# A layer norm in two operations of VectorE, in place of three on ScalarE, GpSimd and VectorE

## The chip, the cores and the metric

The kernel runs on one core of a Trainium2 chip. The time is that of one execution on the device, in microseconds (us); for a kernel on one core it is that core's time. TensorE multiplies matrices into PSUM; VectorE (DVE in the profile), ScalarE (ACT) and GpSimd (POOL) work on tiles in SBUF; SyncE (SP) issues nearly all DMA transfers here. Every engine takes its instructions strictly in the order in which the program lists them: an instruction that waits holds up all that stand behind it on its engine, and that holds for SP's transfers too.

## The reference, cut to what matters

Two groups of tokens ("p", 1024 rows, and "s", 512 rows, each of 1024 channels) go through two layers. A layer is a mixer (attention with a gate), an output projection, and a layer norm over the residual sum:

```python
def _layernorm(h, g, b):
    mu = jnp.mean(h, axis=-1, keepdims=True)
    var = jnp.mean(jnp.square(h - mu), axis=-1, keepdims=True)
    return (h - mu) * lax.rsqrt(var + LN_EPS) * g + b

for l in range(DEPTH):                      # DEPTH = 2
    ...
    u = x * (1 + scale) + shift             # per channel
    y = mixer_a(u, ...) if l == 0 else mixer_b(u, ...)      # ends in (att * silu(z)) @ w_out
    x = _layernorm(DEEPNORM_ALPHA * x + gate * y, ln_g[l], ln_b[l])
```

All is float32. Only the last line's norm is touched by the change.

## The kernel before, in words

The program runs its stages one after the other: layer 0's attention of "s" and of "p", layer 0's output projection of both (`out_layer(0, ...)`, 1805 to 1990 us of the profile), layer 1's attention of both, and layer 1's output projection (`out_layer(1, ...)`, 2560 us to the end). TensorE works through a list of *groups*, each of 24 matmuls into one of two PSUM buffers (`pj`, two buffers: group n + 2 can't start before group n has been taken out of its buffer). Float32 precision comes from splitting each operand into a rounded part and a rest, `hi` and `lo`, hence three matmuls per 128 channels.

In an output projection the rows are cut in 12 *blocks* of 128 rows: block 0 to 3 are "s", 4 to 11 are "p". A block has two groups, c = 0 and c = 1, for the two halves of the 1024 output channels (the first two blocks run crosswise: 0, 1, 0, 1). What belongs to a block:

- `load` (L1033): a DMA of 512 KB, the block's gated attention output, from the scratch tensor `g_s` or `g_p`;
- `split` (L1046, L1047): ScalarE makes `hi`, then VectorE `lo`; TensorE needs both for the block's groups;
- `load_x` (L1037): a DMA of 512 KB, the residual input `x`;
- the *evacuation* of each group by VectorE: y = a * gate (L1070, reads PSUM and so frees it), x = ALPHA x + y (L1071), statistics (L1072);
- the layer norm of the whole block, once both halves are there: `stat` (L1078 to L1086: VectorE joins the statistics to mean and variance `mv`; four tiny operations of GpSimd make rstd in `mv[:, 1:2]` and -mean x rstd in `nm`), `norm` (L1090, ScalarE: x rstd + nm), `scale` (L1094: x g) and `shift` (L1098: x + b). Of even blocks GpSimd does `scale` and VectorE `shift`, of odd ones the other way round;
- the store of the block (L1100), on SP's queue, to the scratch `x_s`, `x_p` after layer 0 (`x_in[r, 1]`) and to the outputs after layer 1. The store waits for `shift`.

The order on every engine is set by *slots*. TensorE's list has six slots per group: one after each four matmuls, and one after the evacuation is listed. `after(n, f)` lists f's work n slots later; `spread(tasks, n)` lists one task of a list per slot. Before a block's first group, `ahead_of(j)` (L1131) sets off, for block j: x of block j + 1 two slots later, the split of block j + 1 five slots later, and the load of block j + 2 eight slots later. After its second group, `then(j)` (L1147) sets off the list of `finish` (L1105), in which `None` is an empty slot; block 0's list has extra empty slots, since the rows g and b of the norm (`ROW`) are loaded in the second step.

In layer 0 block 3's list goes on with the input of layer 1 for "s": `u_make` (L271) transposes all four "s" blocks on TensorE (L275), 128 channels at a time, then ScalarE (L278, L267) and GpSimd (L269) scale and split them. These transposes stand among the matmuls of the groups and need the finished norm of block 3.

Into the first blocks of each output projection falls the end of the last head pair of "p": a small load of factors `f_p` (L767), products with them (L774 on VectorE and L773 on GpSimd in layer 0, L776 in layer 1), L781, L782, the last part of block 4's split (L1053, L1054) and the store L788 of `g_p`, which the loads of blocks 5 to 11 wait for.

The last block of layer 1 has a list of its own, `finish_last` (L1113), in two halves of 512 channels, all on ScalarE and VectorE.

Of the kernel before, what the change touches and what calls it, by code (L numbers as in the profile page):

```python
# [10 lines left out]
F32 = mybir.dt.float32  # L11
F32R = mybir.dt.float32r
AF = mybir.ActivationFunctionType
ALU = mybir.AluOpType

D = 1024
# [59 lines left out]
def trunk(ctx: ExitStack, tc: tile.TileContext, x_p, x_s, c_p, c_s, w_mod, b_mod, ln_g, ln_b,  # L76
          w_in_a, w_out_a, w_in_b, w_out_b, sink_b, pat_d, id_d, y_p, y_s):
    nc = tc.nc
    PSUM = bass.MemoryType.PSUM
    const = ctx.enter_context(tc.tile_pool(name="const", bufs=1))  # L80
    wk = ctx.enter_context(tc.tile_pool(name="wk", bufs=2))
# [44 lines left out]
    def after(n, f):  # L126
        delayed.append((now[0] + n, f))
# [11 lines left out]
    def spread(tasks, slots):  # L139

        q = Queue(tasks, slots)
        queues.append(q)
        return q
# [94 lines left out]
    def u_alloc(r, l, h=None):  # L238

        if h is None:  # L240
            for part in range(2):
                for k in range(NK):
                    U[r, l, part, k] = slabs.get(F32R)
        else:
            for k in range(NK):
                U[r, l, h, k] = slabs.get(F32R, (128, 2, 512))
# [24 lines left out]
    def u_make(r, l, h, k, xs, b0=0):  # L271
        n = len(xs)
        t = ps_t.tile([128, 4, 128], F32, tag="t", name="t")
        for b in range(n):
            nc.tensor.transpose(t[:, b, :], xs[b][:, k * 128:(k + 1) * 128], ident)  # L275
        s = wk.tile([128, 512], F32, tag="stg", name="ustg")[:, :128 * n]
        m = modT[l][:, REQ[r], :]
        nc.scalar.activation(s, t[:, :n].rearrange("p b t -> p (b t)"), AF.Identity,  # L278
                             bias=m[:, k:k + 1], scale=m[:, 8 + k:9 + k])
        u_split(r, l, k, s, 512 * h + 128 * b0, 128 * n)  # L280
# [18 lines left out]
    def chunk(srcs, groups, pre=None, post=None, deep=0, keep=None, how="pool"):  # L299


        plan.append((range(len(loads), len(loads) + len(srcs)), groups, pre, post, deep, keep))
        loads.extend((src, how) for src in srcs)
# [710 lines left out]
    ROW = {}  # L1014

    def load_row(name, ap):
        ROW[name] = slabs.get()
        nc.sync.dma_start(ROW[name], ap.partition_broadcast(128))

    def free_rows(*names):  # L1020
        slabs.put(*(ROW.pop(n) for n in names))

    class Block:
# [54 lines left out]
        def stat(self):  # L1078
            P = nc.gpsimd
            self.mv = mv = wk.tile([128, 2], F32, tag="mv", name="mv", bufs=4)  # L1080
            self.nm = nm = wk.tile([128, 1], F32, tag="nmr", name="nmr", bufs=4)
            nc.vector.bn_aggr(mv, self.s6)
            P.tensor_scalar(nm, mv[:, 0:1], -1.0, 1.0, ALU.mult, ALU.mult)
            P.tensor_scalar(mv[:, 1:2], mv[:, 1:2], EPS, None, ALU.add)
            P.tensor_tensor(mv[:, 1:2], mv[:, 1:2], mhalf, ALU.pow)
            P.tensor_tensor(nm, nm, mv[:, 1:2], ALU.mult)  # L1086

        def norm(self, cs=slice(0, D)):
            x = self.x[:, cs]
            nc.scalar.activation(x, x, AF.Identity, bias=self.nm, scale=self.mv[:, 1:2])  # L1090

        def scale(self, engine, cs=slice(0, D)):
            x = self.x[:, cs]
            engine.tensor_tensor(x, x, ROW["g"][:, cs], ALU.mult)  # L1094

        def shift(self, engine, cs=slice(0, D)):
            x = self.x[:, cs]
            engine.tensor_tensor(x, x, ROW["b"][:, cs], ALU.add)  # L1098
            out = y_out[self.r] if self.l else x_in[self.r, 1]
            nc.sync.dma_start(out[self.t, cs], x)  # L1100

# [2 lines left out]

        def finish(self):  # L1105

            V, P = nc.vector, nc.gpsimd
            e = (V, P) if self.b % 2 else (P, V)
            keep = (self.r, self.l) == ("s", 0)
            return [self.stat, None, None, None, self.norm, None, lambda: self.scale(e[0]), None, None,  # L1110
                    lambda: self.shift(e[1])] + ([] if keep else [self.free])

        def finish_last(self):  # L1113
            V, P = nc.vector, nc.gpsimd
            self.stat()
            parts = [slice(0, 512), slice(512, 1024)]
            for cs in parts:
                self.norm(cs)
            for cs in parts:
                self.scale(V, cs)  # L1120
                self.shift(V, cs)
            self.free()

    def out_layer(l, first, p0):

        w = (w_out_a if l == 0 else w_out_b)[0]
        W = []
        blocks = first + [Block("s", l, b) for b in (2, 3)] + [p0] + [Block("p", l, b) for b in range(1, 8)]
        n = len(blocks)

        def ahead_of(j):  # L1131

            def f():
                if j + 1 < n:
                    after(2, blocks[j + 1].load_x)
                    after(5, (lambda: p0.split(NP - 1)) if blocks[j + 1] is p0 else blocks[j + 1].split)
                if j + 2 < n:
                    k = blocks[j + 2]
                    if k is p0:
                        after(6, lambda: k.load(0, NP - 1))  # L1140
                        after(9, k.alloc)
                        after(11, lambda: load_row("gatep", gate_d["p", l]))
                    else:
                        after(8, k.load)
            return f

        def then(j):  # L1147
            def f():
                k = blocks[j]
                if l == 1 and j == n - 1:  # L1150
                    k.finish_last()
                    return
                t = k.finish()
                if j == n - 1:
                    t.append(lambda: free_rows("g", "b", "gatep"))
                if l == 0 and j == 3:
                    t += [None, lambda: u_alloc("s", 1, 0)]
                    t += [lambda c=c: u_make("s", 1, 0, c, [b.x for b in blocks[:4]]) for c in range(NK)]
                    t.append(lambda: [b.free() for b in blocks[:4]])
                t = [None] * (8 if j == 0 else 1) + t  # L1160
                spread(t, len(t))
                if j == 3:
                    free_rows("gates")
            return f

        def tiles(c):
            return [[(0, 512, w[256 * i:256 * i + 256, 512 * c:512 * c + 512])] for i in range(4)]

        def begin():
            after(1, blocks[1].load_x)  # L1170
            after(8, blocks[2].load)

        def second():
            ahead_of(1)()
            after(11, lambda: load_row("g", ln_g[l]))
            after(11, lambda: load_row("b", ln_b[l]))

        chunk(tiles(0), [blocks[j].group(W, 0, then(j)) for j in range(2)], pre=begin, keep=W, deep=3)
        chunk(tiles(1), [blocks[j].group(W, 1, then(j)) for j in range(2)], pre=second, keep=W, deep=-1)
        for j in range(2, n):  # L1180
            chunk([], [blocks[j].group(W, c, then(j)) for c in range(2)], pre=ahead_of(j), deep=-1,
                  post=(lambda: slabs.put(*(t for p in W for t in p))) if j == n - 1 else None)


    with tc.manual_schedule():
# [133 lines left out]
        for k in range(NK):  # L1319
            t = ps_t.tile([128, 4, 128], F32, tag="t", name="t")  # L1320
# [31 lines left out]
        def shift():  # L1352
            box["m"] = mod_mm(mods[1])

        after(13, shift)
        after(15, lambda: mod_tr(0, 0, box["m"]))
        after(16, whole)
# [35 lines left out]
```

## Time and profile before

| what | value |
|---|---|
| time, median of 3 runs | 2706.53 us (2704.96 to 2712.18) |
| profiled execution, its own time | 2706.52 us |
| span, first to last instruction | 2704.7 us (1.8 us lie around it) |
| mean granted TensorE clock | 0.988 |
| layer norm's full-size operations, ScalarE | L1090: 23 of 128x1024, mean 1244 ns, and 2 of 128x512 |
| on GpSimd | L1094: 12, mean 2451 ns; L1098: 11, mean 2617 ns |
| on VectorE | L1094: 11, mean 1215 ns; L1098: 12, mean 1481 ns; and 2 + 2 of 128x512 |
| GpSimd's tiny ones, 24 each | L1083 696, L1084 300, L1085 630, L1086 328 ns |

How to read it: busy times are per engine and overlap. A row of the timeline gives the start, the duration, the engine, the line of the kernel and what it writes and reads, buffer numbers left out (`s<-s,s` is any slab, `a` a PSUM buffer of a group), `xN` merges N equal instructions that follow each other, and the brackets tell how long the engine was idle before and what ended that. PEclk is the granted share of TensorE's full clock. The windows view gives the busy time of each engine in a stretch, with the number of its instructions.

### The profile page before, as it was taken

Reading aid. Unit: us, or ns where it says so; the run is one execution under the profiler, and the core shown is the slowest. Engines: PE = TensorE matmul, PEld = TensorE weight load, DVE = VectorE, ACT = ScalarE, POOL = GpSimd, SP = SyncE. Lnnn points to the kernel's source line nnn. Section 1 sums busy time; section 2 is a strip of 40 time slices with the busy share of each in tenths; the row PEclk is TensorE's granted clock in tenths of the full one; section 3 lists DMA queues with packets and bytes.
Section 4 is the critical chain, followed back from the end, with each engine's and each line's share of the span. In section 5 each row is a group of like instructions: output and inputs, shape, how many; then the busy total and the mean of one; then the engine's idle time right before and its main releaser. Section 6 shows DMA issues by size and latency. Waiting matters only on the chain.

```text
span 2704.7 us, 39461 instructions
## 1 busy us (share of the span) xinstructions
PE 2610.9 (97%) x15139; PEld 2113.0 (78%) x15139; DVE 1253.9 (46%) x2921; ACT 982.5 (36%) x2359; POOL 945.7 (35%) x662
## 2 busy tenths in 40 slices
PE   7899999999999999999999999999999899999898
PEld 4777778778888887888888888877776678777686
DVE  4533434444243425343433434356645543555666
ACT  3334345543132423233232323242345433444321
POOL 4243334344322323223223231334554531223533
PEclk9899999999999999999999999999999999999999
DMA  8354543333222222122323232335442230211453
GB/s 263 114 147 137 153 98 102 98 98 88 59 56 73 61 56 66 42 66 56 79 56 79 52 75 48 78 118 155 133 135 63 82 91 9 58 47 54 133 170 109
DMA packets 294676, 247.36 MB, mean 91 GB/s; under 512 B 29656, under 2 KB 257880, under 8 KB 294488
## 3 DMA queue, kind: packets, MB, share of 16 engines
q1 hardware_dynamic: 291160, 244.35, 32.2%
q8 instruction: 119, 1.95, 0.3%
q10 hardware_dynamic: 3328, 0.49, 0.1%
q14 instruction: 69, 0.57, 0.1%
HBM read 198.16 MB, written 25.67 MB: 83 GB/s over the span
## 4 chain that ended last, share of the span: by engine, by line
PE 80%; DVE 7%; ACT 4%; issue 3%; POOL 2%; DMA 2%; SPq 0%; ACTq 0%; DVEq 0%; POOLq 0%
PE a L364 62%; PE o L458 6%; PE t L430 5%; PE s L557 2%; PE s L558 2%; DVE nm L416 2%; PE s L562 2%; ACT P L419 1%; DVE P L412 1%; DMA s<-s 1%; POOL s L341 1%; DMA s<-g_s 1%; ACT s L531 1%; DVE s L533 1%; PE t L206 1%
## 5 line engine op out<-in xcount | busy, mean ns | idle before, releaser
L364 PE MATMUL a<-s,s 128*128 128x512 f32 (+1 forms) x9648 | 2128.2, 370 | 23.2 <-POOL s L341 4.7
L364 PEld LDWEIGHTS a<-s,s 128*128 128x128 f32 x9648 | 1615.4, 190 | 317.6 <-issue 29.7
L341 POOL TENSOR_TENSOR s<-s,s 128x1024 fp32r<-128x1024 f32 x211 | 509.7, 2417 | 525.5 <-ACT s L336 258.6
L419 ACT ACTIVATE P<-P,nm 128x256 f32<-128x256 f32 (+2 forms) x576 | 312.3, 543 | 690.4 <-DVE nm L416 677.9
L412 DVE CUSTOM_DVE_ANT_0 P<-s,bias 128x256 f32<-128x256 f32 (+2 forms) x576 | 251.6, 472 | 238.4 <-PE s L558 128.0
L334 POOL TENSOR_SCALAR s<-s 128x1024 fp32r<-128x1024 f32 x139 | 152.5, 1097 | 465.0 <-PE a L364 382.0
L430 PE MATMUL t<-ident,P 128*128 128x128 f32 x1408 | 206.6, 275 | 8.6 <-ACT P L419 3.9
L440 DVE COPY PT<-t 128x256 f32<-128x256 f32 (+3 forms) x320 | 141.7, 447 | 139.8 <-PE t L430 136.9
L533 DVE TENSOR_TENSOR s<-a,s 64x512 fp32r<-64x512 f32 x128 | 109.8, 858 | 203.6 <-ACT s L531 202.5
L430 PEld LDWEIGHTS t<-ident,P 128*128 128x128 f32 x1408 | 166.9, 140 | 44.2 <-ACT P L419 12.2
L458 PE MATMUL o<-PT,s 128*64 128x256 f32 (+1 forms) x1984 | 193.7, 328 | 1.1 <-DVE PT L440 1.1
L458 PEld LDWEIGHTS o<-PT,s 128*64 128x64 f32 x1984 | 118.8, 136 | 87.2 <-issue 49.4
L557 PE MATMUL s<-s,s 128*128 128x256 f32 (+2 forms) x512 | 148.4, 306 | 19.0 <-DVE st L412 18.6
L160 ACT ACTIVATE s<-a 128x128 f32<-128x128 f32 (+2 forms) x147 | 56.0, 407 | 267.1 <-PE a L364 267.0
L558 PE MATMUL s<-s,s 128*128 128x256 f32 (+2 forms) x512 | 144.4, 298 | 3.2 <-DMA s<-s 3.0
L438 ACT ACTIVATE PT<-t 128x256 f32<-128x256 f32 (+3 forms) x320 | 125.9, 398 | 53.1 <-PE t L430 46.9
L542 DVE TENSOR_TENSOR s<-a,s 64x512 fp32r<-64x512 f32 x80 | 77.2, 965 | 132.0 <-ACT s L540 131.0
L557 PEld LDWEIGHTS s<-s,s 128*128 128x128 f32 x512 | 97.7, 191 | 36.7 <-DVE st L412 30.0
L416 DVE TENSOR_SCALAR nm<-st 128x2 f32<-128x2 f32 x288 | 119.0, 413 | 10.0
L162 DVE COPY s<-a 128x128 f32<-128x128 f32 (+2 forms) x105 | 49.4, 491 | 146.4 <-PE a L364 140.6
L531 ACT ACTIVATE s<-a 64x512 fp32r<-64x512 f32 x128 | 100.9, 789 | 26.7 <-PE a L364 25.9
L568 DVE SCALAR_TENSOR_TENSOR s<-th,a 128x512 f32<-128x512 f32 x48 | 43.0, 897 | 143.0 <-ACT th L566 143.0
(112 smaller groups left out, 1667.9 us busy)
## 6 DMA issues: line engine op xcount, KB each, us to landing
s<-in_w_in_a_dram SPq DMA_DIRECT2D x128, 512.0 KB, 5.2
s<-in_w_mod_dram SPq DMA_DIRECT2D x48, 512.0 KB, 7.7
s<-in_w_in_b_dram SPq DMA_DIRECT2D x40, 512.0 KB, 5.5
s<-in_w_in_a_dram SPq DMA_DIRECT2D x64, 256.0 KB, 3.2
s<-s SPq DMA_DIRECT2D x64, 256.0 KB, 4.1
s<-f_p SPq DMA_DIRECT2D x48, 256.0 KB, 5.2
s<-in_x_prompt_dram SPq DMA_DIRECT2D x16, 512.0 KB, 5.7
g_p<-s SPq DMA_DIRECT2D x16, 512.0 KB, 3.4
```

The costliest lines, as they stand in the source:

```text
L334: nc.gpsimd.tensor_scalar(hi, t, 1.0, 1.0, ALU.mult, ALU.mult)
L341: (nc.vector if how == "fast" else nc.gpsimd).tensor_tensor(lo, t, hi.bitcast(F32), ALU.subtract)
L364: nc.tensor.matmul(a, lhsT=lhsT, rhs=rhs, start=(n == 0), stop=(n == 3 * NK - 1))
L412: nc.vector.tensor_tensor_reduce(out=p[:, :s.n], in0=t[:, :s.n], in1=s.bias(h), op0=ALU.add, op1=ALU.max, scale=0.125, scalar=-3e38, accum ...
L416: nc.vector.tensor_scalar(nm, s.st[:, s.b, :, 0], -1.0, None, ALU.mult)
L419: nc.scalar.activation(p[:, :s.n], p[:, :s.n], AF.Exp, bias=nm[:, h:h + 1], accum_out=s.st[:, s.b, h, 1:2])
L430: nc.tensor.transpose(t[0:r0 + n, i, :], s.P[h][:, c0 - r0:c0 + n], ident)
L440: nc.vector.tensor_copy(pt[r0:r0 + n, i:j], t[r0:r0 + n, i:j])
L458: nc.tensor.matmul(o[64 * h:64 * h + 64, cs], lhsT=v(h)[r0:r0 + n, :], rhs=pair.PT[h][r0:r0 + n, blocks, :], start=fresh[steps[0]], stop=stop)
L533: nc.vector.tensor_tensor(w[e][me[1 - e]], f[e](a[me[e]]), w[e][me[e]].bitcast(F32), ALU.subtract)
L557: nc.tensor.matmul(t, lhsT=q, rhs=kk, start=True, stop=False)
L558: nc.tensor.matmul(t, lhsT=q, rhs=kl, start=False, stop=True)
```

## The change

The norm is written as ((x - mean) g) rstd + b. `scale` is now one scalar_tensor_tensor of VectorE, (x - mean) x g with the mean as a value per row, and `shift` another, x rstd + b. ScalarE's `norm` is gone, GpSimd makes only rstd (two tiny operations in place of four), and all full-size operations of all blocks are VectorE's. The list of a block has 7 slots up to `shift` in place of 10, and block 0's list begins two slots later.

```diff
         def stat(self):
             P = nc.gpsimd
             self.mv = mv = wk.tile([128, 2], F32, tag="mv", name="mv", bufs=4)
-            self.nm = nm = wk.tile([128, 1], F32, tag="nmr", name="nmr", bufs=4)
             nc.vector.bn_aggr(mv, self.s6)
-            P.tensor_scalar(nm, mv[:, 0:1], -1.0, 1.0, ALU.mult, ALU.mult)
             P.tensor_scalar(mv[:, 1:2], mv[:, 1:2], EPS, None, ALU.add)
             P.tensor_tensor(mv[:, 1:2], mv[:, 1:2], mhalf, ALU.pow)
-            P.tensor_tensor(nm, nm, mv[:, 1:2], ALU.mult)
-
-        def norm(self, cs=slice(0, D)):
+
+        def scale(self, cs=slice(0, D)):
             x = self.x[:, cs]
-            nc.scalar.activation(x, x, AF.Identity, bias=self.nm, scale=self.mv[:, 1:2])
-
-        def scale(self, engine, cs=slice(0, D)):
+            nc.vector.scalar_tensor_tensor(x, x, self.mv[:, 0:1], ROW["g"][:, cs], ALU.subtract, ALU.mult)
+
+        def shift(self, cs=slice(0, D)):
             x = self.x[:, cs]
-            engine.tensor_tensor(x, x, ROW["g"][:, cs], ALU.mult)
-
-        def shift(self, engine, cs=slice(0, D)):
-            x = self.x[:, cs]
-            engine.tensor_tensor(x, x, ROW["b"][:, cs], ALU.add)
+            nc.vector.scalar_tensor_tensor(x, x, self.mv[:, 1:2], ROW["b"][:, cs], ALU.mult, ALU.add)
             out = y_out[self.r] if self.l else x_in[self.r, 1]
             nc.sync.dma_start(out[self.t, cs], x)
...
         def finish(self):
-            V, P = nc.vector, nc.gpsimd
-            e = (V, P) if self.b % 2 else (P, V)
             keep = (self.r, self.l) == ("s", 0)
-            return [self.stat, None, None, None, self.norm, None, lambda: self.scale(e[0]), None, None,
-                    lambda: self.shift(e[1])] + ([] if keep else [self.free])
+            return [self.stat, None, None, None, self.scale, None, self.shift] + ([] if keep else [self.free])

         def finish_last(self):
-            V, P = nc.vector, nc.gpsimd
             self.stat()
-            parts = [slice(0, 512), slice(512, 1024)]
-            for cs in parts:
-                self.norm(cs)
-            for cs in parts:
-                self.scale(V, cs)
-                self.shift(V, cs)
+            for cs in (slice(0, 512), slice(512, 1024)):
+                self.scale(cs)
+                self.shift(cs)
             self.free()
...
-                t = [None] * (8 if j == 0 else 1) + t
+                t = [None] * (10 if j == 0 else 1) + t
```

In the changed kernel `scale` is at L1087, `shift` at L1091, the joining of the statistics at L1081, and the store at L1093.

**SP's queue, layer 1's output projection, blocks 2 to 4.** L1033 is the 512 KB load of a block's attention output, L1037 that of x, L1100 (before) and L1093 (after) the store of a finished block: the first store below is block 2's (s_16), the loads `g_p` those of blocks 5, 6 and 7. Before:

```order
L1037 DMA s_10_23523<-x_p 128x1024
L1033 DMA s_42_23559<-g_p_81 128x8x128
L1100 DMA out_dram<-s_16_23264 128x1024
L1037 DMA s_11_23599<-x_p 128x1024
L1033 DMA s_4_23637<-g_p_81 128x8x128
L1100 DMA out_dram<-s_21_23411 128x1024
L1037 DMA s_6_23677<-x_p 128x1024
L1033 DMA s_29_23715<-g_p_81 128x8x128
```

After:

```order
L1037 DMA s_10_23464<-x_p 128x1024
L1093 DMA out_dram<-s_16_23216 128x1024
L1033 DMA s_42_23501<-g_p_81 128x8x128
L1037 DMA s_11_23536<-x_p 128x1024
L1093 DMA out_dram<-s_21_23360 128x1024
L1033 DMA s_4_23575<-g_p_81 128x8x128
L1037 DMA s_6_23610<-x_p 128x1024
```

The store, listed three slots earlier, has moved past one load of `g_p`: block 5's load (s_42) stood ahead of block 2's store and stands behind it now, and so on for every block up to the last, in layer 0 as in layer 1.

**VectorE, layer 0's output projection, blocks 3 and 4.** L1082 (before) and L1081 (after) join block 3's statistics, L1047 is the split of block 5, the first L1070 takes out block 4's group c = 0 and the second its group c = 1; the norm's operations on s_39 are block 3's. Before:

```order
L1082 BN_AGGR mv<-s_16853 128x2
L1047 TENSOR_TENSOR s_0_16922<-s_4_16867,s_5_16921 128x1024
L1070 TENSOR_TENSOR ystg<-a,s_40_16798 128x512
L1071 SCALAR_TENSOR_TENSOR s_1_16831<-s_1_16831,ystg 128x512
L1072 BN_STATS s_16931<-s_1_16831 128x6
L1094 TENSOR_TENSOR s_39_16712<-s_39_16712,s_28_16678 128x1024
L1070 TENSOR_TENSOR ystg<-a,s_40_16798 128x512
```

After:

```order
L1081 BN_AGGR mv<-s_16842 128x2
L1047 TENSOR_TENSOR s_0_16907<-s_4_16857,s_5_16906 128x1024
L1087 SCALAR_TENSOR_TENSOR s_39_16709<-s_39_16709,mv,s_28_16678 128x1024
L1070 TENSOR_TENSOR ystg<-a,s_40_16792 128x512
L1071 SCALAR_TENSOR_TENSOR s_1_16820<-s_1_16820,ystg 128x512
L1072 BN_STATS s_16916<-s_1_16820 128x6
L1091 SCALAR_TENSOR_TENSOR s_39_16709<-s_39_16709,mv,s_26_16680 128x1024
L1070 TENSOR_TENSOR ystg<-a,s_40_16792 128x512
```

Where VectorE had one operation of the norm per block between two evacuations, it has two: `scale` (L1087) between the split and the evacuation of c = 0, `shift` (L1091) between the two evacuations. On TensorE the transposes of `u_make` (L275) stand 12 matmuls earlier among the groups than before, since block 3's list is three slots shorter: the first four behind 16 matmuls of block 4's group c = 1, where they stood behind 4 matmuls of block 5's group c = 0. GpSimd's list lost all its full-size operations of the norm, ScalarE's its L1090.

## The prediction

> **What bounds the kernel now.** I read the page's first part, then the windows view over the two output projections, then the timeline of TensorE, since only what holds TensorE up can change the time.
>
> ```profile
> span 2704.7 us, 39461 instructions
> PE 2610.9 (97%) x15139; PEld 2113.0 (78%) x15139; DVE 1253.9 (46%) x2921; ACT 982.5 (36%) x2359; POOL 945.7 (35%) x662
> 1860.00:1880.00 20.00, 16.94 (x68) 13.53 (x67) 14.36 (x15) 3.13 (x4) 11.74 (x8) 0.91 0.57 161
> 2640.00:2660.00 20.00, 20.00 (x90) 16.53 (x90) 14.68 (x18) 4.61 (x4) 7.48 (x10) 1.00 0.51 157
> ```
>
> TensorE is busy for 97% of the span. The two windows are one stretch of each output projection: busy time of PE, PEld, DVE, ACT, POOL, then the granted clock. In layer 1's steady stretch TensorE never pauses, so work taken from ScalarE and GpSimd there is worth nothing by itself; in layer 0's first blocks it loses some 3 us and full clock. Its waits in layer 0's output projection, and the one behind it, are these:
>
> ```profile
> 1873.60 19.22 PE L364 MATMUL a<-s,s 128*128 128x512 f32 x76 [3.06 <-DVE ystg L1070]
> 1895.19 0.33 PE L275 MATMUL t<-ident,s 128*128 128x128 f32 x1 [2.04 <-POOL s L1098]
> 1915.74 71.02 PE L364 MATMUL a<-s,s 128*128 128x512 f32 x312 [1.57 <-DVE ystg L1070]
> 1988.09 1.91 PE L364 MATMUL a<-s,s 128*128 128x256 f32 x14 [1.33 <-DVE s L926]
> 1867.63 2.07 DVE L774 TENSOR_TENSOR s<-s,s 128x1024 f32<-128x1024 f32 x1 [4.67 <-DMA s<-f_p]
> 1869.61 3.34 DVE L1098 TENSOR_TENSOR s<-s,s 128x1024 f32<-128x1024 f32 x1
> 1872.87 0.68 DVE L1070 TENSOR_TENSOR ystg<-a,s 128x512 f32<-128x512 f32 x1
> 1879.61 0.68 DVE L1070 TENSOR_TENSOR ystg<-a,s 128x512 f32<-128x512 f32 x1
> 1870.00:1873.40 3.40, 0.54 (x3) 0.12 (x1) 3.40 (x2) 0.00 (x0) 1.87 (x1) 1.00 0.21 84
> 1874.20:1877.60 3.40, 3.40 (x10) 2.66 (x9) 3.12 (x4) 0.18 (x1) 0.00 (x0) 0.50 0.97 289
> 1877.60:1881.00 3.40, 3.40 (x16) 2.79 (x15) 2.77 (x5) 1.54 (x3) 1.91 (x4) 1.00 0.84 283
> ```
>
> The 3.06 us wait ends with the evacuation at 1872.87, which stood behind an L1098 of 3.34 us. After 2.9 idle us of 3.4 the granted clock is 0.50 for a stretch of 3.4 us (10 matmuls in place of 16), which costs another 1.7.
>
> **The price of the new operations.** A full-size product of VectorE, and the nearest relatives of the new form, with a value per row:
>
> ```profile
> 2634.62 0.69 DVE L1071 SCALAR_TENSOR_TENSOR s<-s,ystg 128x512 f32<-128x512 f32 x1
> L1094 DVE TENSOR_TENSOR s<-s,s 128x1024 f32<-128x1024 f32 x11 | 13.4, 1215 | 1.9 <-ACT s L1090 1.9
> L1292 DVE SCALAR_TENSOR_TENSOR s<-s,modT,s x8: 739/1520/2842, 26.1 to 38.1; 128x512 fp32r<-128x512 f32 x8
> ```
>
> With a constant the half-size form takes 0.69, with a value per row at best 0.74: so 1.215 becomes 1.25 for 1024 elements. The upper end is twice the median of 1.52, 3.0; I take 1.25, since GpSimd then has nothing of full size left beside these blocks. VectorE does 2 x 1.25 per block in place of about 1.2: 1.3 us more of 10.88, with 14.68 of 20 busy before, so its throughput is no bound. ScalarE's and GpSimd's removed operations cost nothing where nobody waits for them.
>
> **What is moved: SP's queue.** The block's list is three slots shorter, so a block's store now stands ahead of the load of the block three further on; before, it stood behind it. The load waits for the store's turn, the store for `shift`. Before, the load issued behind the store of one block earlier, with a block to spare. Now this is a closed loop of one block: `shift` of j - 1, store, load of j + 2, its split, then (behind the split on VectorE) `scale` and the evacuation of block j's first half, `shift` of j. Its rows, from layer 1:
>
> ```profile
> 2639.66 0.34 SPq L1100 DMA_DIRECT2D out_dram<-s  x1
> 2640.04 0.42 SPq L1037 DMA_DIRECT2D s<-x_p  x1
> 2640.52 0.78 SPq L1033 DMA_DIRECT2D s<-g_p  x1
> 2646.45 1.06 ACT L1046 ACTIVATE s<-s 128x1024 fp32r<-128x1024 f32 x1 [1.10 <-DMA s<-g_p]
> 1880.32 0.37 SPq L1033 DMA_DIRECT2D s<-g_p  x1
> 1884.62 1.06 ACT L1046 ACTIVATE s<-s 128x1024 fp32r<-128x1024 f32 x1 [2.95 <-DMA s<-g_p]
> 2570.54 0.34 SPq L788 DMA_DIRECT2D g_p<-s  x1
> 2570.98 0.37 SPq L1033 DMA_DIRECT2D s<-g_s  x1
> s<-g_s SPq DMA_DIRECT2D x1, 512.0 KB, 4.8
> 2632.15 1.18 DVE L1047 TENSOR_TENSOR s<-s,s 128x1024 fp32r<-128x1024 f32 x1
> 2633.89 0.69 DVE L1070 TENSOR_TENSOR ystg<-a,s 128x512 f32<-128x512 f32 x1 [0.56 <-PE a L364]
> 2635.96 1.21 DVE L1094 TENSOR_TENSOR s<-s,s 128x1024 f32<-128x1024 f32 x1
> 2644.77 0.69 DVE L1070 TENSOR_TENSOR ystg<-a,s 128x512 f32<-128x512 f32 x1 [1.96 <-PE a L364]
> ```
>
> SP's step from the store to the next issue is 0.4 (2639.66 to 2640.04); then the landing, X; ScalarE's half of the split 1.06; VectorE's 1.1 until the next operation starts; `scale` 1.2, the same way; evacuation until the norm's next operation 2.07 (2633.89 to 2635.96); `shift` 1.25. That is 7.1 + X. TensorE's period is 10.88 (two groups, 2633.89 to 2644.77). X: a load alone took 4.3 (1880.32 to 1884.62), one behind a store, as here, 4.8, the third in line 5.9 (2640.52 to 2646.45). I take 4.6, between the first two, for x is now issued well ahead of the pair. The loop takes 11.7, **0.8 over the period**.
>
> **Part by part**, against the profiled execution's 2706.52, which is the median (2706.53) for this purpose.
>
> *Layer 0, up to the transposes: +3.0.* Without the slow L1098 (3.34 to 1.25) the evacuation comes at 1870.8: the 3.06 wait and its half clock go. But `scale` of block 2 (1.25) now stands ahead of the next evacuation: 6.74 (1872.87 to 1879.61) and 1.25 further, 1878.8; `shift` ends 3.3 later, 1882.1. The load of block 5 goes at 1882.5, lands at 1887.1; split, `scale`, evacuation (1.06, 1.1, 1.2, 2.07) end at 1892.5, `shift` of block 3 at 1893.8. The transposes that need it resume 1.4 earlier than at 1895.19, yet three slots, 12 matmuls or 2.7 us, earlier in TensorE's list: net +1.3. TensorE starts at 1871.5, has 64 matmuls before them (76 less 12: 14.5 us) and a gap of 2.6 (its next group ends at 1876.9, the buffer it needs is free at 1879.5), so it stands there at 1888.6 and waits 5.2 us, so a half-clock stretch of 1.7 comes with it: +3.0. The Trainium skill, "TensorE: Matmul & The Clock Gate", section on the HAM clock gate, lets only a whole idle window of fixed phase halve the clock; an estimate by it spares the 1.7 in some phases, which would make the whole sum +3.4; the 0.50 row behind 2.9 idle us neither fixes nor denies the phase.
>
> *Layer 0, the rest: -2.6.* The 1.57 wait at 1915.74 was for a `shift` behind GpSimd: -1.6. From there the loop lags by 5 x 0.8 = 4.0 up to the last load, less than the 4.7 which the second PSUM buffer forgives (a group of 5.44 less an evacuation): 0. ScalarE's last norm goes:
>
> ```profile
> 1981.57 1.25 ACT L1090 ACTIVATE s<-s,nmr,mv 128x1024 f32<-128x1024 f32 x1 [8.62 <-POOL nmr L1086]
> 1982.72 0.57 ACT L923 ACTIVATE s<-a 64x512 fp32r<-64x512 f32 x1
> ```
>
> It stood ahead of L923, ScalarE's first work for the next stage, for which VectorE and then TensorE (the 1.33 us at 1988.09) wait: -1.0 (0 to -1.25).
>
> *Layer 1: +6.3.* No slack is left at its start:
>
> ```profile
> 2592.25 1.09 SPq L767 DMA_DIRECT2D s<-f_p  x2
> 2596.81 1.99 DVE L776 TENSOR_TENSOR s<-s,s 128x1024 f32<-128x1024 f32 x1 [3.70 <-DMA s<-f_p]
> 2605.35 0.68 DVE L1070 TENSOR_TENSOR ystg<-a,s 128x512 f32<-128x512 f32 x1
> ```
>
> The factors' loads now queue behind a store, up to 2 us later, against 0.8 that L776 gains beside an idle GpSimd and a `shift` of 1.2 that comes ahead of it; I leave this at nothing. Block 3's first evacuation gets `scale` ahead of it: 2605.35 + 1.25, and the buffer is free at 2607.3. TensorE was ready for it at 2606.7 (the evacuation of 2633.89 waited for TensorE; five groups of 5.44 earlier), so 0.7 is lost. From then on each of seven loads (blocks 5 to 11) costs the whole 0.8: 0.7 + 5.6. At X = 4.3 the layer costs 4.2, at 4.8, 7.7, at 5.9, 15.4.
>
> *The tail: -1.6.*
>
> ```profile
> 2695.91 0.21 DVE L1082 BATCH_NORM_AGGREGATE mv<-s 128x2 f32<-128x12 f32 x1
> 2700.54 0.69 DVE L1098 TENSOR_TENSOR s<-s,s 128x512 f32<-128x512 f32 x1
> ```
>
> Statistics to last sum took 5.3. Now 0.2, then four operations of 0.73, with a wait of about 0.6 for rstd: 3.7 (-1.3 to -2.0).
>
> Sum: 3.0 - 1.6 - 1.0 + 6.3 - 1.6 = **+5.1, 2711.6 us**.
>
> **Rivals.** A measurement of this kernel tells about 0.3%, 8.1 us, from no change.
>
> *The loop turns slower (slower, 0.33).* If the load lands as late as in the third-in-line row, X is above 4.6. Each 0.1 costs 0.7 in layer 1, and beyond 4.8 another 0.5 in layer 0, where the buffer forgives no more. It decides from X = 4.9; at 5.3: 3.7 + 2.8 - 1.6 - 1.0 + 11.2 - 1.6 = +13.5, 2720. For it: the load at 2640.52, amid the steady stretch, took 5.9. Against it: x is no longer between.
>
> *The loop is hidden (no change, 0.13).* With X at 3.8 it fits 10.88: 2.2 - 1.6 - 1.0 + 0.7 - 1.6 = -1.3, 2705.2. Against it: no load's row is under 4.3.
>
> *GpSimd was the brake (faster, 0.14).* Beside GpSimd's product VectorE's operations stretch:
>
> ```profile
> 2645.43 2.40 POOL L1094 TENSOR_TENSOR s<-s,s 128x1024 f32<-128x1024 f32 x1 [1.35 <-ACT s L1090]
> 2645.50 2.88 DVE L1071 SCALAR_TENSOR_TENSOR s<-s,ystg 128x512 f32<-128x512 f32 x1
> ```
>
> 2.88 for 0.69. If that, and not the loads, is what delayed block norms, all of layer 0's waits go without a successor: -3.06 - 1.7 - 2.04 - 1.57, with -1.0 and -1.6, makes -11.0, 2695.5. The Trainium skill, "SBUF — State Buffer", section "Who interferes with whom", speaks for it: GpSimd and VectorE's second pair of ports lock each other out; these two rows agree. Against it: TensorE is busy throughout the window of layer 1 that holds this pair.
>
> That the change does not do what it says would show as new operations at 3.0 each: 3.5 more in the loop, slower by far; I count it in the first rival.
>
> **The numbers.** My forecast (X 4.3 to 4.9) has 0.40, the rivals 0.33, 0.13 and 0.14. Faster 0.14; within 0.3% 0.53; slower 0.33. The range leaves out most of the faster rival and the slow rival's upper third: 2700 to 2722.
>
> **What would show it.** Right: L1033 issues 0.4 behind L1093 in every block; layer 1's evacuations (L1070) of first halves 11.7 apart, with a TensorE wait in each; TensorE idle some 5 us near 1888 ahead of L275, with PEclk at half; L1087 and L1091 at 1.25; the tail at 3.7. Wrong: layer 1's period still 10.88, or loads landing under 4.

## The result and the profile after

The changed kernel takes 2725.34 us (median of 4 runs, 2724.24 to 2726.91), the kernel before 2706.62 in the same comparison: ratio 1.0064, 95% interval 1.0052 to 1.0077, **18.7 us slower**. The forecast was 2711.6 us with a range of 2700 to 2722, so the time lies outside the range, on the side of the first rival.

From the page of the changed kernel, the span and the busy times:

```profile
span 2723.5 us, 39349 instructions
PE 2616.3 (96%) x15139; PEld 2113.6 (78%) x15139; DVE 1265.6 (46%) x2944; ACT 953.3 (35%) x2334; POOL 866.6 (32%) x591
```

GpSimd lost 79 us of work and ScalarE 29, VectorE gained 12: the change does what it says. TensorE has the same 15139 matmuls and waits longer. The timeline of TensorE in the changed kernel, the groups that waited, in layer 0 and then in layer 1:

```profile
1873.81 5.78 PE L364 MATMUL a<-s,s 128*128 128x512 f32 x24 [0.96 <-DVE ystg L1070]
1881.85 9.33 PE L364 MATMUL a<-s,s 128*128 128x512 f32 x40 [2.26 <-DVE ystg L1070]
...
1897.65 0.48 PE L275 MATMUL t<-ident,s 128*128 128x128 f32 x1 [6.15 <-DVE s L1091]
...
1909.08 6.63 PE L364 MATMUL a<-s,s 128*128 128x512 f32 x28
1916.78 11.17 PE L364 MATMUL a<-s,s 128*128 128x512 f32 x48 [1.07 <-DVE ystg L1070]
1930.08 11.12 PE L364 MATMUL a<-s,s 128*128 128x512 f32 x48 [2.13 <-DVE ystg L1070]
1941.97 11.13 PE L364 MATMUL a<-s,s 128*128 128x512 f32 x48 [0.77 <-DVE ystg L1070]
...
2618.85 11.17 PE L364 MATMUL a<-s,s 128*128 128x512 f32 x48 [1.04 <-DVE ystg L1070]
2630.69 11.16 PE L364 MATMUL a<-s,s 128*128 128x512 f32 x48 [0.67 <-DVE ystg L1070]
...
2702.68 11.12 PE L364 MATMUL a<-s,s 128*128 128x512 f32 x48 [0.83 <-DVE ystg L1070]
```

From 1916.78 on each row shown is 48 matmuls, one block, and begins with a wait. In layer 1 seven blocks take 2702.68 - 2618.85 = 83.83 us, 11.98 each. In the kernel before the same seven take 76.47, 10.92 each, out of a row without a wait:

```profile
2589.67 104.03 PE L364 MATMUL a<-s,s 128*128 128x512 f32 x456
```

To see where the time went I took the same place on TensorE's list in both traces (by the count of all its instructions) and the difference of the starts, stretch by stretch. In the table, positive is longer than in the kernel before, and stretches are named by that kernel's times; the experiments below it are set against the same profile.

| kernel | layer 0 up to the transposes, 1838.9 to 1903.4 | layer 0, the rest, to 1988.1 | layer 1, 2571.7 to 2693.7 | tail |
|---|---|---|---|---|
| the change | +4.1 | +4.9 | +9.3 | -1.4 |
| e1 all loads first | -2.9 | -1.0 | -0.3 | -1.4 |
| e2 old slots | -2.2 | -3.2 | -0.3 | -1.4 |
| e3 old operations, short list | +8.2 | +11.7 | +15.3 | +2.0 |
| e4 two stores | +5.7 | +4.7 | +10.4 | -1.6 |
| e5 store on ScalarE's queue | -2.4 | -0.9 | -0.3 | -1.7 |
| e6 x between | +5.7 | +13.0 | +22.4 | -1.4 |
| e7 loads first in layer 1 | +2.2 | +5.4 | -0.4 | -1.4 |
| e8 transposes late | -1.0 | +1.3 | +9.1 | -1.4 |
| e9 split early | +3.9 | +4.1 | +8.9 | -1.3 |
| e10 tail only | +1.4 | -1.4 | +0.1 | -1.3 |
| e11 block 2's load first | -2.4 | +5.3 | +9.2 | -1.4 |
| e12 loads first in layer 0 | -2.2 | -0.9 | +9.5 | -1.3 |

The four stretches of the change make 16.9 of the 18.75 us between the two spans; the other 1.9 lie in stretches that the change doesn't touch, which differ by a few us from one execution to the next. Row e10, which differs from before in the tail alone, shows how far a single stretch scatters: 1.4. The change and e7 run the same code up to the transposes, and differ there by 1.9. The border inside layer 0 is soft, since the change moves the transposes: by the count of the groups' matmuls alone the change has +5.2 and +3.8, with the same sum.

The loop itself, one turn of it in layer 1, from the changed kernel's timelines of SP, ScalarE and VectorE:

```profile
2645.33 0.34 SPq L1093 DMA_DIRECT2D out_dram<-s  x1
2645.77 0.38 SPq L1033 DMA_DIRECT2D s<-g_p  x1
2646.25 0.99 SPq L1037 DMA_DIRECT2D s<-x_p  x1
```

```profile
2650.32 1.06 ACT L1046 ACTIVATE s<-s 128x1024 fp32r<-128x1024 f32 x1 [10.71 <-DMA s<-g_p]
```

```profile
2644.04 1.27 DVE L1091 SCALAR_TENSOR_TENSOR s<-s,mv,s 128x1024 f32<-128x1024 f32 x1
...
2651.42 1.23 DVE L1047 TENSOR_TENSOR s<-s,s 128x1024 fp32r<-128x1024 f32 x1 [3.81 <-ACT s L1046]
2652.56 1.28 DVE L1087 SCALAR_TENSOR_TENSOR s<-s,mv,s 128x1024 f32<-128x1024 f32 x1
2653.76 0.68 DVE L1070 TENSOR_TENSOR ystg<-a,s 128x512 f32<-128x512 f32 x1
...
2655.81 1.27 DVE L1091 SCALAR_TENSOR_TENSOR s<-s,mv,s 128x1024 f32<-128x1024 f32 x1
```

`shift` ends at 2645.31, the store issues in the same moment, the load 0.44 later (SP's issue before these had ended at 2635.1, so the load stood there for some 10 us behind the waiting store); it lands after 4.55, and split, `scale`, evacuation and the next `shift` follow without a gap: 2644.04 to 2655.81 is one turn, 11.77. VectorE stands idle for 3.81 us of it, ScalarE for 10.71: no engine is short of time, the turn is.

### The profile page after: what moved, and what is told of

It is laid out like the page before. It is cut to its first block, busy times and chain, and to the rows that moved or that the text cites. A ratio compares the mean times of both kernels' runs of the same rounds, so it can differ in the third digit from the quotient of the medians.

```text
span 2723.5 us, 39349 instructions
## 1 busy us (share of the span) xinstructions
PE 2616.3 (96%) x15139; PEld 2113.6 (78%) x15139; DVE 1265.6 (46%) x2944; ACT 953.3 (35%) x2334; POOL 866.6 (32%) x591
## 4 chain that ended last, share of the span: by engine, by line
PE 72%; DVE 11%; DMA 5%; ACT 5%; issue 3%; POOL 1%; SPq 0%; ACTq 0%; POOLq 0%; DVEq 0%
PE a L364 55%; PE o L458 6%; PE t L430 5%; DMA s<-g_p 2%; PE s L557 2%; PE s L558 2%; DVE nm L416 2%; ACT P L419 2%; PE s L562 2%; DVE P L412 1%; DMA s<-s 1%; DVE s L1087 1%; DVE s L1091 1%; POOL s L341 1%; ACT s L1046 1%
```

## The experiments

Theory: the store ahead of the load on SP's queue closes this loop, and the loop is the loss. First rival: VectorE's two operations, `scale` ahead of the evacuation above all, are the loss, whatever SP's order.

### e1: the load ahead of the store again

```diff
-    ... self.scale, None, self.shift] + ([] if keep else [self.free])      # shift ends with the store
+    ... self.scale, None, lambda: (self.shift(), after(3, put))] + ...     # put: the store, then free
```

> The changed kernel with one thing put back: the store of a block is listed three slots after its shift, so that on SP's queue the load of the block three further on stands ahead of it again. All other work, the slots of scale and shift and of the transposes, stays as in the changed kernel. Queue theory (the loop shift, store, load, split, scale, evacuation, shift is what costs): the loop is cut, TensorE has no wait in layer 1 behind the first blocks (saves 9.2 us), none in the regular blocks of layer 0 (6.0), and the wait of 6.15 us ahead of layer 0's transposes falls below 2 us: 2701 to 2708 us. Rival (the two operations on VectorE, above all scale listed ahead of the evacuation, are what delays TensorE, and the order of SP does not matter): 2723 to 2727 us, waits in every block as before.

Measured: 2704.46 against 2704.33 us, ratio 0.9994 (0.9983 to 1.0005). The same window of layer 1 as in the prediction, in the changed kernel and then in this one:

```profile
2640.00:2660.00 20.00, 18.43 (x81) 14.64 (x80) 15.22 (x20) 1.06 (x1) 1.22 (x4) 1.00 0.35 109
```

```profile
2640.00:2660.00 20.00, 20.00 (x90) 16.57 (x89) 13.96 (x18) 2.12 (x2) 4.07 (x4) 1.00 0.41 126
```

TensorE is at 18.43 of 20 in the one and full in the other, with the same operations on VectorE. In layer 0 the wait ahead of the transposes is 1.10 in place of 6.15; of the waits behind it, which were to go, one of 1.48 is left. The rival is out.

### e2: the new operations at the old slots

```diff
-    [self.stat, None, None, None, self.scale, None, self.shift]                            # block 0: 10 empty slots
+    [self.stat, None, None, None, self.scale, None, None, None, None, self.shift]          # block 0: 8, as before
```

> The two new operations at the slots of the old list: scale where the old norm stood, shift and store where they stood before the change. SP's order is that of the kernel before, and the transposes stand where they stood before. Queue theory: about 2702 to 2706 us, period of layer 1's blocks 10.88 us, the tail shorter by 1.3 us. VectorE rival: still some 10 to 19 us above the kernel before, 2717 to 2725 us, since the same operations are all on VectorE.

Measured: 2699.43 us, ratio **0.9973 (0.9959 to 0.9986)**: faster than both, and below the forecast of 2702 to 2706. Of TensorE's four waits in layer 0 (3.06, 2.04, 1.57 and 1.33) only the first is left, in two parts:

```profile
1875.36 7.34 PE L364 MATMUL a<-s,s 128*128 128x512 f32 x24 [2.22 <-DVE ystg L1070]
1883.40 12.05 PE L364 MATMUL a<-s,s 128*128 128x512 f32 x52 [0.70 <-DVE ystg L1070]
```

The wait at the transposes and that behind GpSimd's product are gone, and layer 0's two stretches are 5.4 us shorter than before. So the two operations on VectorE, taken alone, are worth a gain; the order that came with them cost some 25 us (from a ratio of 0.9973 to 1.0064).

### e3: the old operations in the short list

```diff
-    [self.stat, None, None, None, self.norm, None, lambda: self.scale(e[0]), None, None, lambda: self.shift(e[1])]
+    [self.stat, None, None, None, self.norm, lambda: self.scale(e[0]), lambda: self.shift(e[1])]
```

> The kernel before with its old operations on three engines, but with the list shortened to the 7 slots of the change (norm, scale and shift in successive slots), so that stores and transposes stand in SP's and TensorE's order as in the changed kernel. Queue theory: the loop exists here too, and is longer by ScalarE's norm and GpSimd's products (each 2.4 us in place of 1.25): slower than the changed kernel, 2728 to 2745 us, waits in every block of layer 1. VectorE rival: no more than 3 us from the kernel before, 2704 to 2710 us.

Measured: 2743.01 us, ratio 1.0148 (1.0119 to 1.0177). The short list alone, with not one new operation, costs more than twice what the change costs. The wait ahead of the transposes:

```profile
1896.87 0.47 PE L275 MATMUL t<-ident,s 128*128 128x128 f32 x1 [9.52 <-POOL s L1098]
```

### e4: one more issue in the loop

```diff
-    nc.sync.dma_start(out[self.t, cs], x)
+    for c in (left half of cs, right half of cs): nc.sync.dma_start(out[self.t, c], self.x[:, c])
```

> The changed kernel with each block's store cut in two transfers of 512 columns, both ahead of the load: one more issue of 0.4 us on SP inside the loop, the same bytes. Queue theory: the period of layer 1's blocks grows from 11.97 by 0.4 us, and over 7 periods there and 6 in layer 0 the time grows by about 5 us, 2729 to 2732 us. VectorE rival, and any theory in which SP's queue is not in the loop: 2724 to 2727 us, no change.

Measured: 2729.80 us, ratio 1.0088 (1.0068 to 1.0108), inside the forecast, but not for my reason: layer 1's blocks take 11.93 us on average (seven, 2623.81 to 2707.32), no longer than the change's. One turn, SP and ScalarE:

```profile
2661.82 0.81 SPq L1095 DMA_DIRECT2D out_dram<-s  x2
2662.72 0.39 SPq L1033 DMA_DIRECT2D s<-g_p  x1
```

```profile
2666.96 1.06 ACT L1046 ACTIVATE s<-s 128x1024 fp32r<-128x1024 f32 x1 [10.86 <-DMA s<-g_p]
```

The load issues 0.90 after the store and not 0.44, and lands 4.24 after its issue and not 4.55. Counted from the store's issue it is 5.14 against 4.99, and over layer 1's seven loads 5.1 on average in both runs: the second issue did not make the load later, as if the bytes that stand ahead set the landing and the issue were hidden behind them. The dose that I had chosen was next to none, so this run decides little; its interval overlaps the change's.

### e5: the stores on another queue

```diff
-    nc.sync.dma_start(out[self.t, cs], x)
+    nc.scalar.dma_start(out[self.t, cs], x)
```

> The changed kernel with the stores of the blocks issued from ScalarE's queue; SP then carries the loads alone and no load waits for a shift. The slots, the operations and the bytes are those of the changed kernel; ScalarE waits for each shift ahead of its next split. If it is SP's strict order that makes the loads late: no wait in layer 1's regular blocks (period 10.88 us), the wait ahead of the transposes under 3 us, ratio to the kernel before 0.996 to 1.001. If it is the store's bytes that delay the load on the DMA engines, or the operations on VectorE: 1.004 to 1.007, as the changed kernel.

Measured: 2702.95 against 2704.89 us, ratio 0.9996 (0.9981 to 1.0010). The same slots, operations and bytes; the stretches are those of e1. What made the loads late is their place behind the waiting store on SP's queue. This run takes the store's wait and its bytes out of that queue together and does not part them; in the turn above the wait was some 10 us, and the change's loads of layer 1 landed 4.7 us after their issue on average, against 4.3 for one alone, so the bytes are the small part.

### e6: x between the store and the load

```diff
-    after(8, k.load)
+    after(15, k.load)
```

> The changed kernel with the load of a block's attention output listed seven slots later, so that SP issues store, x, load in place of store, load, x. Same transfers, same operations. The loop then has one more issue (0.48 us) and the landing of a transfer third in line, 5.5 to 6.0 us in the kernel before, in place of 4.7: queue theory: period of layer 1's blocks 13.2 to 13.6 us in place of 11.97, and with 7 such blocks there and 6 in layer 0 some 16 to 22 us more than the changed kernel, ratio 1.0125 to 1.015. If two stores gave no change because the landing counts from the store and not from the issues, this still adds the bytes of x ahead of the load: at least 1 us per block. Any theory without the loop: within 2 us of the changed kernel, 1.006 to 1.007.

Measured: 2745.93 us, ratio 1.0147 (1.0132 to 1.0163), at the upper end of the forecast. A turn, on SP and ScalarE, and two of TensorE's blocks:

```profile
2642.95 0.34 SPq L1093 DMA_DIRECT2D out_dram<-s  x1
2643.34 0.42 SPq L1037 DMA_DIRECT2D s<-x_p  x1
2643.82 0.78 SPq L1033 DMA_DIRECT2D s<-g_p  x1
```

```profile
2649.55 1.06 ACT L1046 ACTIVATE s<-s 128x1024 fp32r<-128x1024 f32 x1 [12.33 <-DMA s<-g_p]
```

```profile
2640.43 12.72 PE L364 MATMUL a<-s,s 128*128 128x512 f32 x48 [2.45 <-DVE ystg L1070]
2653.82 11.14 PE L364 MATMUL a<-s,s 128*128 128x512 f32 x48 [0.67 <-DVE ystg L1070]
```

The load lands 6.60 after the store's issue and not 4.99, 1.6 more, and the period is 13.39 (2640.43 to 2653.82) in this turn. Over layer 1's seven loads it is 7.0 against 5.1 on average, 1.8 more, and the period is 13.8 (a little above the forecast) against 12.0, longer by the same 1.8. (The 12.72 is TensorE at a reduced clock, see the last section; the next block waits the less, so it is the loop that sets the period.) Nothing but the order of two transfers was changed. This is the dose that e4 had missed.

### e7 and e12: one layer each

```diff
+    last = (lambda: (self.shift(), after(3, put))) if self.l == 1 else (lambda: (self.shift(), put()))    # e12: self.l == 0
```

> The store listed three slots later, behind the load, in layer 1 alone; layer 0 stays as in the changed kernel. Queue theory with the layers' prices read from the trace of the changed kernel (9.3 us in layer 1, 9.0 in layer 0 with its handover): layer 1's output projection back to the length of before, layer 0's still 9 us longer, the tail 1.3 shorter: 7 to 9 us above the kernel before, ratio 1.0025 to 1.0035.

> The store behind the load in layer 0 alone, the counterpart of the run with layer 1 alone. By the prices read from the traces (layer 0 falls from 9.0 above the kernel before to 3 to 4 below it; layer 1 stays 9.3 above; the tail 1.4 below): 3 to 6 us above the kernel before, ratio 1.001 to 1.002. If the two layers' losses are not independent (the loop of layer 1 hangs on what layer 0 leaves behind): off that by more than 3 us.

Measured: e7 2713.58 us, ratio 1.0035 (1.0023 to 1.0046); e12 2712.29 us, 1.0028 (1.0017 to 1.0039), somewhat above its forecast of 1.001 to 1.002. Cutting the loop in one layer takes out that layer's loss and leaves the other's as it was (the table: 9.5 in layer 1 with layer 0 cut; 7.6 in layer 0 with layer 1 cut): within the scatter of a stretch the two are independent, and they are of like size.

### e8, e9 and e11: what costs in layer 0

Layer 0 was forecast at 0.4 us and came out at 9.0. e8 lists the transposes three slots later, where they stood before; e9 moves one split on ScalarE; e11 one store.

```diff
-    t += [None, lambda: u_alloc("s", 1, 0)]                 # e8
+    t += [None] * 4 + [lambda: u_alloc("s", 1, 0)]
-    after(5, ... blocks[j + 1].split)                       # e9
+    after(2 if (l, j) == (0, 5) else 5, ... blocks[j + 1].split)
+    # e11: after(3, put) for layer 0's block 2 alone
```

> The changed kernel with the transposes of layer 0's block 3 listed three slots later, where they stood among TensorE's matmuls before the change. If their early place is what costs in layer 0: the wait ahead of them falls from 6.15 to about 3.4 us, too short for a half-clock stretch of full length, and 3 to 5 us are saved, ratio 1.0045 to 1.0055. If the loop alone decides layer 0: what is saved there is lost again in the following blocks, because the transposes then keep ScalarE from the next split just as long after block 3's shift: 0 to 1.5 us saved, 1.006 to 1.0065.

> The changed kernel with one operation moved: in layer 0 the split of block 6 is listed three slots earlier, so that on ScalarE it stands behind four of the eight transposed channels, as before the change, and not behind seven. The transposes keep their early place and TensorE its wait ahead of them. If that split's place is what used up the slack of the regular blocks of layer 0 (it started at 1911.2, 8.7 us after its load had landed): it starts some 4 us earlier, block 4's shift ends as much earlier, the 1.1 and 2.1 us waits that follow shrink, and 3 to 6 us of the 18.7 are saved: ratio 1.004 to 1.0055. If the wait ahead of the transposes and the loop alone cost it: within 1 us of the changed kernel, 1.006 to 1.007.

> The changed kernel with one store moved: that of layer 0's block 2 is listed three slots later, behind the load of block 5; all other blocks of both layers keep the store ahead of the load. Block 3's shift, which the transposes need, then no longer waits for a load that itself waited for a shift. If TensorE's wait ahead of the transposes (6.15 us and its half clock) is the larger part of layer 0's loss: it falls to 1 to 2 us, as in the run with all loads first (1.10), and the split of block 6 comes earlier by as much; 5 to 8 us are saved, ratio 1.0035 to 1.0045. If layer 0's loss belongs to the loop of its regular blocks, which then only begins earlier: at most 2 us saved, 1.0057 or more.

Measured: e8 2716.89 us, ratio 1.0041 (1.0025 to 1.0056); e9 2723.99 us, 1.0079 (1.0064 to 1.0094); e11 2720.38 us, 1.0055 (1.0036 to 1.0074). In the changed kernel the split of block 6 stood here on ScalarE, with VectorE behind it:

```profile
1911.20 1.04 ACT L1046 ACTIVATE s<-s 128x1024 fp32r<-128x1024 f32 x1
```

```profile
1912.27 1.47 DVE L1047 TENSOR_TENSOR s<-s,s 128x1024 fp32r<-128x1024 f32 x1 [7.22 <-ACT s L1046]
1913.66 2.36 DVE L1087 SCALAR_TENSOR_TENSOR s<-s,mv,s 128x1024 f32<-128x1024 f32 x1
1915.95 0.68 DVE L1070 TENSOR_TENSOR ystg<-a,s 128x512 f32<-128x512 f32 x1
```

Its load had issued at 1898.04 and was in SBUF at 1902.5 (the last of its sixteen completions in the trace). It waited behind seven of the eight transposed channels, which ScalarE scales; in the kernel before, it stood behind four. With the transposes late (e8) it starts at 1901.98, TensorE's wait ahead of them is 0.43, and layer 0 gives back 8.7 of its 9.0 us, more than forecast. Not all of that is the transposes' place: the change's load of block 5 landed 1.5 us later than e8's (last section), and the clock was full behind the change's wait of 2.26 us ahead of the same blocks and reduced behind e8's. e7, with the change's code in layer 0, has the load on time and the reduced clock as e8 has them. Its rows:

```profile
1880.47 10.96 PE L364 MATMUL a<-s,s 128*128 128x512 f32 x40 [2.31 <-DVE ystg L1070]
...
1894.81 0.47 PE L275 MATMUL t<-ident,s 128*128 128x128 f32 x1 [3.06 <-DVE s L1091]
```

Against e7's 7.6, e8's 0.3 gives the transposes' early place 7.3 us; by the times of the runs e8 is 6 us below the change (1.0041 against 1.0064). But the split's place is not the cause by itself. e9 starts it at 1901.51 and saves nothing that can be told. Counted from the first transpose behind the wait, the split starts 5.0 us earlier than in the change and the evacuation behind it only 1.4, for the next wait in line takes over:

```profile
1909.84 0.69 DVE L1070 TENSOR_TENSOR ystg<-a,s 128x512 f32<-128x512 f32 x1 [4.58 <-POOL s L269]
```

The evacuation waits for GpSimd's work on the transposes: both take their staging tile from one set of two buffers (the tag "stg" in the code). A row of e8 has it the other way round, ScalarE's `ustg` waiting for VectorE's L1071, which reads `ystg`; nothing else ties these two together. A run with buffers of their own was not made.

```profile
1909.22 0.78 ACT L278 ACTIVATE ustg<-t,modT 128x512 f32<-128x512 f32 x1 [2.02 <-DVE s L1071]
```

And e11 removes TensorE's wait at the transposes altogether (its stretch falls from +4.1 to -2.4), and the rest of layer 0 stays at +5.3; its ratio can't be told from the change's, its trace shows 6.1 us less in layer 0. So my expectation that the split's place used up the slack fell. What holds is that the early transposes, with all that they put ahead of a block's split and evacuation, are worth some 7 of layer 0's 9.0 us while the loop is closed; how these part between the split and the staging tiles stays open. With the loop cut they are worth at most the 1.5 us between layer 0 in e1 and in e2, about the one wait of 1.48 that e1 still has there and e2 has not.

### e10: the tail alone

```diff
     # finish_last of the kernel before, with the two new operations; all other blocks as before
...
+    V.scalar_tensor_tensor(x, x, self.mv[:, 0:1], ROW["g"][:, cs], ALU.subtract, ALU.mult)
+    V.scalar_tensor_tensor(x, x, self.mv[:, 1:2], ROW["b"][:, cs], ALU.mult, ALU.add)
...
```

> The kernel before with the two new operations in the last block's list alone: all other blocks keep ScalarE's norm and the alternating products and sums. In the five profiles with the new tail, statistics to the end of the span shrank by 1.3 to 1.7 us: 1.4 us less than the kernel before, ratio 0.9995, which a measurement can hardly tell from 1. If the old_slots version owes its gain of 7 us to the tail, this run would show 0.9975; if to the work taken from GpSimd and ScalarE in layer 0 (5.4 us by its trace), 0.9995.

Measured: 2705.50 us, ratio 1.0005 (0.9994 to 1.0015): no change that can be told, and its trace has the tail 1.3 shorter. So the tail is 1.3 us of e2's gain of 7; the 5.4 in its layer 0 are the larger part by its trace.

## Why the prediction was wrong

By its own steps:

- **The price of the operations** was right: 1.25 forecast, 1.28 and 1.27 measured (L1087, L1091 above); beside GpSimd's part of the transposes, which the forecast did not count, one took 2.36 (at 1913.66).
- **The moved store and the loop** were right, in mechanism and in most of the size. Landing X: 4.6 forecast; seven loads of layer 1 landed after 4.5 to 5.1, mean 4.7. Period: 11.7 forecast, 11.98 measured, so 1.1 over and not 0.8.
- **Layer 0 up to the transposes: +3.0** forecast, +4.1 measured, +2.2 in e7, which runs the same code there. The mechanism held, its size in part by luck. The wait ahead of the transposes was forecast at 5.2 and is 6.15; 1.5 of it is the load of block 5, which landed after 6.05 and not 4.6, and in e7, with that load on time and 1.6 of the wait taken up by the reduced clock ahead of it, it is 3.06. The clock was halved behind the wait, as forecast; this row of the changed kernel's windows has it (0.50, 11 matmuls):

```profile
1897.60:1901.00 3.40, 3.35 (x11) 2.76 (x12) 0.00 (x0) 1.68 (x3) 1.27 (x1) 0.50 0.76 229
```

- **Layer 0, the rest: -2.6 forecast, +4.9 measured. This is the step that failed**, 7.5 us of the 13.6 that were missing. The two savings came (the 1.57 us wait is gone, and ScalarE's last norm: TensorE's lag falls by 1.2 at the handover), but "the loop lags by 5 x 0.8 = 4.0 up to the last load, less than the 4.7 which the second PSUM buffer forgives" did not hold: TensorE waits in every block, 1.07, 2.13 (1.5 of it the second late load), 0.77 and so on. The slack had been granted from block 5 on, as if that block's evacuation came when TensorE was ready. It came at 1915.95, 6 us after the group's end (its last four matmuls begin the row at 1909.08), so the slack was gone before the first lag. The transposes, three slots earlier, had used it up: with them back in their place (e8) this stretch is +1.3. I had followed them on TensorE's list and not on ScalarE's and GpSimd's, which they move on too, ahead of the split and of the staging tiles; which of these two weighs more stays open (e9).
- **Layer 1: +6.3 forecast, +9.3 measured**: 7.4 over the seven blocks in place of 5.6; 1.3 at the first of them in place of 0.7 (by the forecast's own figures 0.6); and 0.6 ahead of that. The last I put down to the factors' loads behind a store, which I had left at nothing. They issued behind it at 2605.14, and L776 started 13.4 later than before where the stage stood 10.9 later:

```profile
2605.14 1.26 SPq L767 DMA_DIRECT2D s<-f_p  x2
```

```profile
2610.19 1.23 DVE L776 TENSOR_TENSOR s<-s,s 128x1024 f32<-128x1024 f32 x1 [2.87 <-DMA s<-f_p]
```

- **The tail: -1.6** forecast, -1.4 measured: from 2716.01 to 2719.95, 3.9 in place of 5.3.

```profile
2716.01 0.21 DVE L1081 BATCH_NORM_AGGREGATE mv<-s 128x2 f32<-128x12 f32 x1
...
2719.20 0.75 DVE L1091 SCALAR_TENSOR_TENSOR s<-s,mv,s 128x512 f32<-128x512 f32 x1
```

The first rival gave the sign, and a small part of the cause: in layer 1 X was 4.7 on average, short of its 4.9; in layer 0 two late loads make it 5.0, 1.5 us each. The last rival, GpSimd as the brake, was priced with the loop left out: e2, where the order is kept, is 7 us faster, of the 11 that it gave; e2 relieves ScalarE too and does not part the two.

## What to carry to other kernels

Shortening a list of tasks moves every instruction that the later tasks issue, on every queue: follow each of them on each engine, transfers first. A store that waits for its data, listed ahead of a load on the same strict queue, ties the load to the work behind it; check whether the chain from that load leads back to the same store, and compare its length with the stage's period. Where a slack is to absorb a lag, show from rows that the slack is there at the point where the lag begins.

## What the runs showed of the hardware

- In layer 1 a load of 512 KB directly behind a store of 512 KB was there 4.9 to 5.5 us after the store's issue, whether the store was one transfer or two (5.1 on average in the change and in e4); with another 512 KB between them (e6), 6.6 to 7.7.
- In layer 0 of the change two loads landed after 6.05 and 6.12 and not 4.5 (issues at 1884.78 and 1919.67). The second is as late in e3, e7, e9 and e11 (5.9 to 6.4), and not in e8 (4.6); the first is late in e3 and e9 (6.0), and not in e7 and e8 (4.6). Of the sixteen completions of each late load fifteen are on time and one is 1.3 to 1.9 late, and each time a 16 KB transfer of the queue that the profile calls "instruction" began 3.06 to 3.86 us after the load's issue and took 1.0 to 1.6 us. No load directly behind a store that came on time has one so placed; in e7 and e8 it began 3.89 and 3.88 after the issue of the first. The coincidence speaks for this transfer as the cause; no run moves it. The change's DMA view of 1884.7 to 1891 has it (it began at 1888.58), the view of 1898 to 1902.6, with the load on time, has no such line:

```profile
q8 instruction: 1, 0.02, 1.2%
```

- A wait of 2.45 us of TensorE was followed by a block at reduced clock (12.72 us, e6 above), one of 2.39 in the same run was not (11.14, below). Ahead of the same 40 matmuls of layer 0 a wait of 2.26 to 2.31 us stands in nine of the runs: in the change, e1 and e9 they took 9.3 us behind it, in e4, e5, e6, e7, e11 and e12 10.9 to 11.0. The Trainium skill, "TensorE: Matmul & The Clock Gate", section on the HAM clock gate, says that the activity is judged in free-running windows of about 3.4 us; a dependence on the phase agrees with these rows, but none of these waits fills such a window, so a window need not be idle from end to end:

```profile
1955.92 11.14 PE L364 MATMUL a<-s,s 128*128 128x512 f32 x48 [2.39 <-DVE ystg L1070]
```
